# Rotating the latent-attention queries half by half, and transposing score maxima seven matmul groups after their reduction

## The chip, the cores and the metric

One core of a Trainium2 chip runs the whole program. The metric is the device time of one execution in microseconds (us). Three runs of the kernel before gave 1178.66, 1180.37 and 1183.4 us; the median is 1180.37.

## The reference, cut to what matters

Two layers run over a sequence of 1024 positions and a width of 1024. In each layer one projection feeds three mixers: retention, latent attention (MLA, 8 heads) and gated linear attention. Each is gated by a silu, and one output matrix follows. The change touches MLA:

```python
q = (rms_norm(q_lat, q_norm_w) @ w_uq).reshape(b, s, MLA_HEADS, MLA_NOPE + MLA_ROPE)
q_nope = q[..., :MLA_NOPE]
q_pe = rope(q[..., MLA_NOPE:], pos)
...
sc = (jnp.einsum('bqhd,bkhd->bhqk', qn, k_nope)
      + jnp.einsum('bqhd,bkd->bhqk', qp, k_pe)).astype(jnp.float32) * scale
mask = key_chunk[None, :] <= q_chunk[:, None]
sc = jnp.where(mask, sc, -jnp.inf)
p = jax.nn.softmax(sc, axis=-1).astype(v.dtype)
```

with `rope` returning `[x1*cos - x2*sin, x2*cos + x1*sin]`. Of each query's 96 columns, 64 ("nope") are used as they are and 32 are rotated.

## The kernel before

Float32 products are made of three matmuls: each operand is split into a high part and the rest, and `mm3` (L556 to L558) sums high*high, high*low and low*high into a PSUM bank. A "group" below is such a set of matmuls that ends in a `tick()`.

The order of TensorE's (PE's) instructions is written by hand, in the order of the Python calls. VectorE (DVE), ScalarE (ACT) and GpSimd (POOL) get their orders from a scheduler; SyncE (SP) starts all transfers, in one queue. Long side jobs are generators, *tasks*: each says after how many ticks of the main stream its next piece is to be put in, and `drain` puts in all that is left at once. In `layer()` the stretch that matters runs so:

- retention's core (`ret_core`) is a task, with one step about every 6 ticks. A step's matmuls (L790 to L834) need from DVE decay products (`retc_ram`, L793), a key product (`retc_rks`, L804) and states (`mq_rst`, L823, L825), and from POOL scaled queries (`retc_rqs`, L798).
- `mla_queries` is a generator that is called twice. The first part makes the rotary queries, two tiles for each half of the sequence (512 positions), and copies them to SBUF (`qx`). Then rz0, a gate projection, runs. The second part rotates both halves (`q_rope`: L732 to L737 on DVE, a cast L1118, the low part on POOL L1119, writes to DRAM L1121) and makes eight nope groups, each evicted by `pair_out` (L1106 on ACT, L1107 on DVE, writes L1109). These groups use PSUM pool `pj`, which has two banks. Then comes rz1.
- POOL also splits weights (L457) for the projections that come next: `wrz` for rz0 and rz1, `wgk` after them.
- `mla_max` is a task that finds, for each head and 128 queries, the maximum of each score row from the high parts: matmuls (L1243) into two sets of PSUM banks, each reduced by DVE (L1245) into a column of `mx`. Twelve such matmuls make one head, with 128 to 512 columns. A piece comes every 1.15 ticks (`MAXW`). The generator `close` then sums up a head's columns (`m8`, L1211), waits for some ticks, and transposes `m8` on PE (L1215) into a row in DRAM (L1217, L1218). It is called before the third block of the next head; for the last head it is a task of its own.
- `drain(big)` puts in what is left of the maxima, behind gate projection mz3 and ahead of the values (`mv`, evicted by L1189) and the attention itself.

Of the kernel before, what the change touches and what calls it, by code (L numbers as in the profile page):

```python
# [162 lines left out]
class Builder:  # L163
# [903 lines left out]
    def mla_queries(self, l, ql, tab):  # L1067

        nc = self.nc
        w, wn = self.weight((l, "uq"))  # L1070
        self.lab = "mq_"
        x = [[], []]
        for hf in range(2):
            for i in range(2):
                ps = self.ps("pj")
                self.uq_mtile(w, ql, i, hf, ps)
                x[hf].append(self.pt(name="qx"))
                nc.scalar.copy(x[hf][i], ps)
        yield
        for hf in range(2):  # L1080
            self.q_rope(l, x[hf], hf, *tab[hf])
        self.lab = "mq_"
        for pr in range(4):
            for hf in range(2):
                ps = self.ps("pj")
                self.uq_mtile(wn, ql, pr, hf, ps)
                self.pair_out(self.qn[l], pr, hf, ps)

    def mla_keys(self, l, kvl):
        (wh, wl), = self.weight((l, "ukvk"))  # L1090
        self.lab = "mk_"
        for pr in range(4):
            for hf in range(2):
                ps = self.ps(("pj", "s")[hf])
                g, cs = kvl[hf], slice(128 * pr, 128 * pr + 128)
                self.mm3(ps, wh[:, cs], wl[:, cs], g[:, 0, :], g[:, 1, :], True, True)
                self.tick()
                self.pair_out(self.kn[l], pr, hf, ps)
        for hf in range(2):
            self.nc.sync.dma_start(self.ld[l][hf], kvl[hf].bitcast(F32))  # L1100
# [92 lines left out]
    def mla_max(self, l):  # L1193

        nc = self.nc
        self.lab = "mmax_"
        sets = [{n: self.sl(dt=F32R, name="mx" + n) for n in "qk"} for _ in range(2)]
        for st in sets:
            for i, n in enumerate("kq"):
                nc.sync.dma_start(st[n][96:104, :].bitcast(F32), self.mrows[i, 1:9])  # L1200
            nc.sync.dma_start(st["k"][64:96, :].bitcast(F32), self.kr[l][0])

        def load(h):
            self.lab = "mmax_"
            for n in "qk":
                self.head_rows(l, h, n, 0, sets[h % 2][n])

        def close(h, mx):
            self.lab = "mmax_"
            m8 = self.sm([128, 8])  # L1210
            nc.vector.tensor_reduce(m8, mx, AX.X, ALU.max)  # L1211
            yield 4
            self.lab = "mmax_"
            ps = self.ps()
            nc.tensor.matmul(ps[0:8, 0:128], m8, self.cst("ident"), start=True, stop=True)  # L1215
            mr = self.smp.tile([8, 128], F32R, tag="mr", name=self.nm("mr"), bufs=2)
            nc.scalar.activation(mr, ps[0:8, 0:128], AF.Copy, scale=-1.0)  # L1217
            nc.sync.dma_start(self.mxd[l][h].rearrange("o (a b) -> (o a) b", a=8), mr.bitcast(F32))  # L1218

        load(0)  # L1220
        done = None
        for h in range(MH):
            yield MAXW
            st = sets[h % 2]
            if h + 1 < MH:
                load(h + 1)
            self.lab = "mmax_"
            mx = self.smp.tile([128, 8, 2], F32, tag="mx", name=self.nm("mx"), bufs=2)
            nc.gpsimd.memset(mx, NEG)
            for i in range(8):  # L1230
                n = 128 * (i + 1)
                for j in range((n + 511) // 512):
                    if i or j:
                        yield MAXW
                    if i == 2 and done:
                        yield from close(*done)
                        done = None
                        yield MAXW
                    self.lab = "mmax_"
                    w = min(512, n - 512 * j)  # L1240
                    ps = self.ps(self.maxp[self.nmx % len(self.maxp)])
                    self.nmx += 1
                    nc.tensor.matmul(ps[:, :w], st["q"][0:104, 128 * i:128 * i + 128],  # L1243
                                     st["k"][0:104, 512 * j:512 * j + w], start=True, stop=True)
                    nc.vector.tensor_reduce(mx[:, i, j:j + 1], ps[:, :w], AX.X, ALU.max)  # L1245
            done = (h, mx)
        self.task(close(*done), 8)

    def mla_scores(self, h, hf, j):
# [337 lines left out]
```

## Time and profile before

| what | value |
|---|---|
| median of three runs | 1180.37 us |
| the profiled execution's own time | 1183.94 us |
| its span | 1182.2 us |
| mean granted TensorE clock | 0.978 of 2.4 GHz |
| PE busy | 1118.6 us (95%) |
| DVE busy | 785.9 us (66%) |
| ACT busy | 596.2 us (50%) |
| POOL busy | 525.8 us (44%) |

The span is that of the profiled execution, from its first to its last instruction. Busy times count each engine by itself, and they overlap. An idle stretch is put down to the instruction that released the waiting one. The granted clock is a share of full speed: 1.00 is 2.4 GHz, 0.50 is 1.2 GHz. Layer 0 and layer 1 run the same program, about 568 us apart.

### The profile page before, as it was taken

What the parts mean: (1) busy time and instruction counts of PE and PEld (TensorE: products, weight loads), DVE (VectorE), ACT (ScalarE), POOL (GpSimd) and SP (SyncE); (2) the same over time, 40 slices, a digit from 0 to 9 for tenths busy, and PEclk for the clock granted to TensorE, in tenths of its full rate; (3) what the DMA queues carried; (4) which work ended last, traced back from release to release, by engine and by line L of the source; (5) the groups of instructions that cost most, each with busy time, mean ns of one, the idle gap of its engine ahead of it and who ended that gap; (6) DMA issues with size and microseconds to landing.
All of it is one profiled execution on the core that took longest, in us unless ns stands there. A gap on an engine that the chain in (4) does not pass through costs nothing.

```text
span 1182.2 us, 16973 instructions
## 1 busy us (share of the span) xinstructions
PE 1118.6 (95%) x5968; PEld 933.9 (79%) x5968; DVE 785.9 (66%) x1366; ACT 596.2 (50%) x1164; POOL 525.8 (44%) x459
## 2 busy tenths in 40 slices
PE   6999996899999999999999999969999999999996
PEld 3878985688878788887787898748888878888896
DVE  6866666568765656868875476474866565686754
ACT  6434342243554678863543434324355557886431
POOL 0055152445433446683565333335453344668620
PEclk8899998899999999999999999989999999999999
DMA  9725661662137534238443356155211653424722
GB/s 370 257 87 161 203 223 54 213 194 73 41 96 216 130 90 108 64 134 311 178 167 101 113 169 239 38 213 150 63 59 41 199 130 90 108 63 156 255 88 72
DMA packets 65585, 169.01 MB, mean 143 GB/s; under 512 B 10262, under 2 KB 13334, under 8 KB 65500
## 3 DMA queue, kind: packets, MB, share of 16 engines
q1 hardware_dynamic: 65500, 167.93, 44.8%
q8 instruction: 47, 0.77, 0.3%
q14 instruction: 38, 0.31, 0.1%
HBM read 125.36 MB, written 38.41 MB: 139 GB/s over the span
## 4 chain that ended last, share of the span: by engine, by line
PE 75%; DVE 12%; DMA 5%; ACT 4%; issue 3%; POOL 1%; SPq 0%; DVEq 0%; POOLq 0%; ACTq 0%
PE mhead_psacc L1294 3%; PE mhead_psacc L1292 3%; PE mhead_psacc L1293 3%; PE pmz_pspj L556 3%; PE pmz_pspj L557 2%; PE pmz_pspj L558 2%; DMA ada_aw<-awc 2%; DVE mmax_mx L1245 2%; PE wo_pss L558 2%; PE wo_pspj L556 2%; PE wo_pss L556 2%; PE wo_pss L557 2%; PE wo_pspj L558 2%; PE wo_pspj L557 2%; PE mhead_pss L1260 2%
## 5 line engine op out<-in xcount | busy, mean ns | idle before, releaser
L457 POOL TENSOR_TENSOR wwo_wl<-wwo_wst,wwo_wh 128x1024 fp32r<-128x1024 f32 x27 | 69.4, 2575 | 39.0 <-ACT wwo_wh L456 38.9
L1245 DVE TENSOR_REDUCE mmax_mx<-mmax_psmm 128x1 f32<-128x512 f32 (+1 forms) x96 | 57.4, 598 | 34.9 <-PE mmax_psmm L1243 33.9
L1269 POOL TENSOR_TENSOR mhead_wh<-mhead_p,mhead_wh 128x384 fp32r<-128x384 f32 (+1 forms) x48 | 57.9, 1207 | 45.5 <-DVE mhead_wh L1268 39.9
L576 DVE SCALAR_TENSOR_TENSOR ada_aw<-ada_aw,silrow 128x512 f32<-128x512 f32 x64 | 60.6, 966 | 18.6 <-DMA ada_aw<-awc 18.4
L1274 DVE TENSOR_TENSOR mhead_ph<-mhead_pss,mhead_ph 128x512 fp32r<-128x512 f32 x48 | 33.0, 688 | 36.2 <-ACT mhead_pss L1273 35.7
L556 PE MATMUL pmz_pspj<-mkh_h,wmz_wh 128*128 128x512 f32 x128 | 53.3, 417 | 0.0
L1269 POOL TENSOR_TENSOR mhead_wl<-mhead_p,mhead_wl 128x128 fp32r<-128x128 f32 (+1 forms) x48 | 35.8, 746 | 34.7 <-DVE mhead_wl L1268 34.7
L557 PE MATMUL pmz_pspj<-mkh_h,wmz_wh 128*128 128x512 f32 x128 | 50.9, 397 | 0.0
L558 PE MATMUL pmz_pspj<-mkh_h,wmz_wl 128*128 128x512 f32 x128 | 50.6, 395 | 0.0
L556 PE MATMUL mq_pspj<-latn_lat,wuq_wh 128*128 128x512 f32 x48 | 21.6, 450 | 26.0 <-DVE mq_pl L1107 25.6
L558 PE MATMUL wo_pspj<-gran_mx,wwo_wl 128*128 128x512 f32 (+1 forms) x120 | 44.3, 369 | 1.9 <-POOL wwo_wl L457 1.9
L556 PE MATMUL wo_pss<-gran_mx,wwo_wh 128*128 128x512 f32 (+1 forms) x120 | 44.5, 371 | 0.0
L556 PE MATMUL wo_pspj<-gran_mx,wwo_wh 128*128 128x512 f32 (+1 forms) x120 | 44.5, 371 | 0.0
L557 PE MATMUL wo_pss<-gran_mx,wwo_wh 128*128 128x512 f32 (+1 forms) x120 | 44.1, 368 | 0.0
L557 PE MATMUL wo_pspj<-gran_mx,wwo_wh 128*128 128x512 f32 (+1 forms) x120 | 44.1, 368 | 0.0
L558 PE MATMUL wo_pss<-gran_mx,wwo_wl 128*128 128x512 f32 (+1 forms) x120 | 44.1, 368 | 0.0
L457 POOL TENSOR_TENSOR wrk_wl<-wrk_wst,wrk_wh 128x1024 fp32r<-128x1024 f32 x3 | 8.0, 2682 | 79.5 <-ACT wrk_wh L456 79.5
L600 ACT ACTIVATE ssq_sq<-ssq_x 128x512 f32<-128x512 f32 (+1 forms) x31 | 16.6, 534 | 50.9 <-DVE ssq_x L1371 50.9
L605 DVE TENSOR_TENSOR ssq_sq<-ssq_sq,ssq_sq 128x512 f32<-128x512 f32 (+1 forms) x30 | 30.9, 1029 | 13.6 <-ACT ssq_sq L600 13.6
L1272 ACT ACTIVATE mhead_ph<-mhead_pss 128x512 fp32r<-128x512 f32 x48 | 28.6, 596 | 17.8 <-PE mhead_pss L1262 17.3
L1243 PE MATMUL mmax_psmm<-mmax_mxk,mmax_mxq 104*128 104x512 f32 (+1 forms) x96 | 35.5, 370 | 2.0 <-DVE mmax_mx L1245 1.5
L556 PE MATMUL pv_pspj<-wgv_wh,mkh_h 128*128 128x256 f32 x128 | 37.0, 289 | 0.0
(560 smaller groups left out, 4124.7 us busy)
## 6 DMA issues: line engine op xcount, KB each, us to landing
ada_aw<-awc SPq DMA_DIRECT2D x64, 256.0 KB
wwo_wst<-wo SPq DMA_DIRECT2D x32, 512.0 KB
aw<-awc SPq DMA_DIRECT2D x11, 512.0 KB
x<-xT SPq DMA_DIRECT2D x8, 512.0 KB
kn<-mk_ph SPq DMA_DIRECT2D x16, 256.0 KB
kn<-mk_pl SPq DMA_DIRECT2D x16, 256.0 KB
qn<-mq_ph SPq DMA_DIRECT2D x16, 256.0 KB
qn<-mq_pl SPq DMA_DIRECT2D x16, 256.0 KB
```

The lines of the kernel that those rows point to most:

```text
L457: (eng or nc.gpsimd).tensor_tensor(lo, src, hi.bitcast(F32), ALU.subtract)
L556: mm(ps, lh, rh, start=start, stop=False)
L557: mm(ps, lh, rl, start=False, stop=False)
L558: self.last = mm(ps, ll, rh, start=False, stop=stop)
L576: step = nc.vector.scalar_tensor_tensor(v, v, 1.0, self.silrow[:, cs], ALU.mult, ALU.mult, accum_out=t[:, 2 * j + i:2 * j + i + 1])
L1243: nc.tensor.matmul(ps[:, :w], st["q"][0:104, 128 * i:128 * i + 128], st["k"][0:104, 512 * j:512 * j + w], start=True, stop=True)
L1245: nc.vector.tensor_reduce(mx[:, i, j:j + 1], ps[:, :w], AX.X, ALU.max)
L1269: nc.gpsimd.tensor_tensor(pl, p, ph.bitcast(F32), ALU.subtract)
L1274: nc.vector.tensor_tensor(pl, s, ph.bitcast(F32), ALU.subtract)
L1292: mm(acc[:, o], vh, ph, start=(j == 0), stop=False, skip_group_check=True)
L1293: mm(acc[0:64, o], vl, ph, start=False, stop=False, skip_group_check=True)
L1294: mm(acc[:, o], vh, pl, start=False, stop=last, skip_group_check=True)
```

## The change

The rotation of the first half is issued in the first part of `mla_queries`, right behind that half's two tiles, ahead of rz0; the rotation of the second half is issued behind the eight nope groups. In `close`, the transposition of a head's maxima comes seven ticks after their last reduction instead of four.

```diff
--- before.py
+++ after.py
@@ -1076,15 +1076,17 @@
                 self.uq_mtile(w, ql, i, hf, ps)
                 x[hf].append(self.pt(name="qx"))
                 nc.scalar.copy(x[hf][i], ps)
+            if hf == 0:
+                self.q_rope(l, x[hf], hf, *tab[hf])
+                self.lab = "mq_"
         yield
-        for hf in range(2):
-            self.q_rope(l, x[hf], hf, *tab[hf])
         self.lab = "mq_"
         for pr in range(4):
             for hf in range(2):
                 ps = self.ps("pj")
                 self.uq_mtile(wn, ql, pr, hf, ps)
                 self.pair_out(self.qn[l], pr, hf, ps)
+        self.q_rope(l, x[1], 1, *tab[1])
 
     def mla_keys(self, l, kvl):
         (wh, wl), = self.weight((l, "ukvk"))
@@ -1209,7 +1211,7 @@
             self.lab = "mmax_"
             m8 = self.sm([128, 8])
             nc.vector.tensor_reduce(m8, mx, AX.X, ALU.max)
-            yield 4
+            yield 7
             self.lab = "mmax_"
             ps = self.ps()
             nc.tensor.matmul(ps[0:8, 0:128], m8, self.cst("ident"), start=True, stop=True)
```

Lines from L1079 on are two further on in the changed kernel. Three places show what moves.

DVE around the nope groups, before (`mrope` and `mq_qx` are the rotation, `mq_pl` the evictions), from the end of the second half's rotation:

```order
L737 TENSOR_TENSOR mq_qx_1610<-mq_qx_1610,mrope_rb_1785 128x512
L735 TENSOR_TENSOR mq_qx_1570<-mq_qx_1570,mrope_ra_1784 128x512
L1118 CAST mrope_qrh_1792<-mq_qx_1570 128x512
L1118 CAST mrope_qrh_1798<-mq_qx_1610 128x512
L793 TENSOR_TENSOR retc_ram_1817<-retc_pss_1811,cst 128x2x128
L793 TENSOR_TENSOR retc_ram_1817<-retc_pss_1812,cst 128x2x128
L804 TENSOR_TENSOR retc_rks_1826<-retc_psmm_1823,cst 128x256
L862 TENSOR_REDUCE hnorm_sm_1845<-hnorm_hsq_1843 128x8
L1107 TENSOR_TENSOR mq_pl_1856<-mq_pspj_1804,mq_ph_1855 128x512
L1107 TENSOR_TENSOR mq_pl_1869<-mq_pspj_1861,mq_ph_1868 128x512
```

DVE in the changed kernel, from retention's second step on:

```order
L804 TENSOR_TENSOR retc_rks_1550<-retc_psmm_1547,cst 128x256
L732 TENSOR_TENSOR mrope_ra_1563<-mq_qx_1561,pv_tab_1323 128x512
L733 TENSOR_TENSOR mrope_rb_1564<-mq_qx_1552,pv_tab_1323 128x512
L736 TENSOR_TENSOR mq_qx_1561<-mq_qx_1561,pv_tab_1322 128x512
L734 TENSOR_TENSOR mq_qx_1552<-mq_qx_1552,pv_tab_1322 128x512
L737 TENSOR_TENSOR mq_qx_1561<-mq_qx_1561,mrope_rb_1564 128x512
L735 TENSOR_TENSOR mq_qx_1552<-mq_qx_1552,mrope_ra_1563 128x512
L823 COPY mq_rst_1532<-retc_psmm_1616 64x64 x2
L823 COPY mq_rst_1533<-retc_psmm_1616 64x64 x2
L1120 CAST mrope_qrh_1571<-mq_qx_1552 128x512
L1120 CAST mrope_qrh_1577<-mq_qx_1561 128x512
L793 TENSOR_TENSOR retc_ram_1605<-retc_pss_1599,cst 128x2x128
```

The rotation of the first half moved from behind rz0 to between two steps of retention, with that step's state copies among it and the next step's products behind. That of the second half stands behind the last two evictions `mq_pl`, with two small norm rows and three state updates in it, and ahead of the last two `retc_ram`.

POOL at the weight splits of rz0 and rz1, before:

```order
L457 TENSOR_TENSOR wrz_wl_1518<-wrz_wst_1461,wrz_wh_1517 128x1024
L798 TENSOR_TENSOR retc_rqs_1588<-prk_rh_666,cst 128x128
L798 TENSOR_TENSOR retc_rqs_1588<-prk_rh_671,cst 128x128
L457 TENSOR_TENSOR wrz_wl_1614<-wrz_wst_1521,wrz_wh_1613 128x1024
L798 TENSOR_TENSOR retc_rqs_1647<-prk_rh_666,cst 128x128
```

and in the changed kernel:

```order
L457 TENSOR_TENSOR wrz_wl_1518<-wrz_wst_1461,wrz_wh_1517 128x1024
L457 TENSOR_TENSOR wrz_wl_1634<-wrz_wst_1521,wrz_wh_1633 128x1024
L1121 TENSOR_TENSOR mrope_qrl_1572<-mq_qx_1552,mrope_qrh_1571 128x512
L1121 TENSOR_TENSOR mrope_qrl_1578<-mq_qx_1561,mrope_qrh_1577 128x512
L798 TENSOR_TENSOR retc_rqs_1608<-prk_rh_666,cst 128x128
```

The two splits now follow each other, and the first half's two low parts stand behind them and ahead of the scaled queries. The second half's two low parts stand likewise ahead of the last pair of `retc_rqs`, behind the split of `wgk`.

PE at `drain(big)` in layer 0, changed kernel, from the seventh head's last maxima (`mxk_2241`) to the last head's (`mxk_2243`):

```order
L1245 MATMUL mmax_psmm_3833<-mmax_mxk_2241,mmax_mxq_2240 128x512
L1245 MATMUL mmax_pss_3836<-mmax_mxk_2241,mmax_mxq_2240 128x512
L1245 MATMUL mmax_psmm_3841<-mmax_mxk_2243,mmax_mxq_2242 128x128
L1245 MATMUL mmax_pss_3844<-mmax_mxk_2243,mmax_mxq_2242 128x256
L1217 MATMUL mmax_psmm_3849<-cst,mmax_sm_3847 8x128
L1245 MATMUL mmax_psmm_3854<-mmax_mxk_2243,mmax_mxq_2242 128x384
L1245 MATMUL mmax_pss_3857<-mmax_mxk_2243,mmax_mxq_2242 128x512
L1245 MATMUL mmax_psmm_3860<-mmax_mxk_2243,mmax_mxq_2242 128x512
```

Before, ten maxima stood in one piece there, all of the last head. Now ten of the head before it, two of the last head, the transposition and the same ten stand in one piece, 22 maxima, ahead of the values.

## Rows read from the trace of the kernel before

**Rows 1.** Page, part 1: busy us, share of the span, instructions, by engine.

```profile
PE 1118.6 (95%) x5968; PEld 933.9 (79%) x5968; DVE 785.9 (66%) x1366; ACT 596.2 (50%) x1164; POOL 525.8 (44%) x459
```

**Rows 2.** Waits of PE: line, what released it, us in total, times, longest.

```profile
PE mq_pspj L556 <- DVE mq_pl L1107: 25.6, 4, 12.5
...
PE mmax_psmm L1215 <- DVE mmax_sm L1211: 3.7, 3, 2.1
...
PE prz_pspj L556 <- DVE mq_pl L1107: 2.3, 2, 1.2
```

**Rows 3.** Timeline of PE, `mq_pspj` and the drain's start: start, us, operation, [idle before].

```profile
210.13 0.80 PE L556 MATMUL mq_pspj<-latn_lat,wuq_wh 128*128 128x512 f32 x1 [12.53 <-DVE mq_pl L1107]
...
214.14 0.53 PE L556 MATMUL mq_pspj<-latn_lat,wuq_wh 128*128 128x512 f32 x1
...
400.44 0.39 PE L558 MATMUL pmz_pspj<-mkh_h,wmz_wl 128*128 128x512 f32 x1
...
400.67 0.34 PE L1243 MATMUL mmax_psmm<-mmax_mxk,mmax_mxq 104*128 104x384 f32 x1
...
778.07 0.79 PE L556 MATMUL mq_pspj<-latn_lat,wuq_wh 128*128 128x512 f32 x1 [12.53 <-DVE mq_pl L1107]
...
780.80 0.51 PE L556 MATMUL mq_pspj<-latn_lat,wuq_wh 128*128 128x512 f32 x1
```

**Rows 4.** Timeline of DVE during PE's first stall.

```profile
201.15 1.75 DVE L732 TENSOR_TENSOR mrope_ra<-mq_qx,pv_tab 128x512 f32<-128x512 f32 x1
...
204.49 0.68 DVE L736 TENSOR_TENSOR mq_qx<-mq_qx,pv_tab 128x512 f32<-128x512 f32 x1
...
207.01 0.76 DVE L1118 CAST mrope_qrh<-mq_qx 128x512 fp32r<-128x512 f32 x2
...
208.81 0.68 DVE L862 TENSOR_REDUCE hnorm_sm<-hnorm_hsq 128x8 f32<-128x512 f32 x1
```

**Rows 5.** Timelines of ACT (first row) and DVE where the halves now go.

```profile
170.41 0.59 ACT L1078 COPY mq_qx<-mq_pspj 128x512 f32<-128x512 f32 x1 [1.44 <-PE mq_pspj L558]
...
174.80 0.97 DVE L823 COPY mq_rst<-retc_psmm 64x64 f32<-64x64 f32 x4
...
227.26 1.29 DVE L1107 TENSOR_TENSOR mq_pl<-mq_pspj,mq_ph 128x512 fp32r<-128x512 f32 x2
```

**Rows 6.** Timeline of POOL around the three places.

```profile
170.52 2.39 POOL L457 TENSOR_TENSOR wrz_wl<-wrz_wst,wrz_wh 128x1024 fp32r<-128x1024 f32 x1
...
201.04 2.97 POOL L1119 TENSOR_TENSOR mrope_qrl<-mq_qx,mrope_qrh 128x512 fp32r<-128x512 f32 x2 [3.31 <-DVE mrope_qrh L1118]
...
228.49 2.39 POOL L457 TENSOR_TENSOR wgk_wl<-wgk_wst,wgk_wh 128x1024 fp32r<-128x1024 f32 x1 [9.60 <-ACT wgk_wh L456]
```

**Rows 7.** Timeline of PE: retention's steps that follow, and the first maxima.

```profile
180.43 0.61 PE L815 MATMUL retc_psmm<-pv_v,retc_rks 128*128 128x128 f32 x4
...
181.72 0.66 PE L834 MATMUL retc_psacc<-mq_rst,retc_rqs 128*128 128x128 f32 x4
...
237.57 1.00 PE L830 MATMUL retc_psacc<-pv_v,retc_ram 128*128 128x64 f32 x8
...
251.71 0.23 PE L1243 MATMUL mmax_psmm<-mmax_mxk,mmax_mxq 104*128 104x128 f32 x1
```

**Rows 8.** Timeline of PE behind the drain, layer 0.

```profile
407.44 0.39 PE L556 MATMUL mv_pspj<-wukvv_wh,pmz_lat 128*128 128x256 f32 x1 [1.52 <-DVE pmz_vl L1189]
```

**Rows 9.** Timeline of DVE in the drain, first reduction and the values' eviction.

```profile
401.05 0.56 DVE L1245 TENSOR_REDUCE mmax_mx<-mmax_psmm 128x1 f32<-128x384 f32 x1 [0.38 <-PE mmax_psmm L1243]
...
406.71 1.28 DVE L1189 TENSOR_TENSOR pmz_vl<-mv_pspj,pmz_vh 128x512 fp32r<-128x512 f32 x2
```

**Rows 10.** Windows: us, busy of PE, PEld, DVE, ACT, POOL, PEclk, DMA share, GB/s.

```profile
404.00:407.00 3.00, 1.92 (x14) 1.67 (x13) 3.00 (x6) 1.59 (x3) 0.57 (x1) 1.00 0.95 249
...
27.50:30.00 2.50, 1.45 (x4) 1.16 (x5) 2.37 (x4) 1.80 (x3) 0.00 (x0) 0.50 1.02 419
...
40.00:42.50 2.50, 2.50 (x16) 2.16 (x15) 2.50 (x5) 0.00 (x0) 0.00 (x0) 0.93 1.03 383
```

## The prediction

> **What bounds the kernel now.** I read the page's busy times first. TensorE (PE) is busy 95% of the span, VectorE (DVE) 66%, GpSimd (POOL) 44% [rows 1]. So a change pays only where it shortens PE's idle time, or costs where it adds some. The next view is therefore the list of what PE waits for [rows 2]. Its largest entry is the one that the change aims at: the third group of the nope queries (`mq_pspj`) waits for the eviction `mq_pl`, 25.6 us in 4 waits, the longest 12.5. The transposition of maxima, which the change also touches, waits 3.7 us in 3 places. In the same list the first group of rz1 (`prz`) waits 2.3 us, in 2 waits, for the last `mq_pl`: a plain wait for one of the two `pj` banks, with nothing foreign in between. That is what a nope group costs when only its own eviction is ahead.
>
> PE's timeline gives the place: idle 12.53 us before 210.13, the same before 778.07 in layer 1 [rows 3]. What DVE does meanwhile is the third view [rows 4]: the rotation of both halves, 16 instructions, whose last casts end at 207.77; behind them retention's products and a norm's sum (208.81), and only then the evictions. The rotation stands ahead of the first eviction in DVE's order, and PE has two banks, so it fills both and stops. The stall has a tail: after it the matmuls come 0.43 us apart instead of 0.23 (400.44 to 400.67 in the same group of rows). In layer 0 nine intervals take 4.01 us (210.13 to 214.14), which at 0.23 would be 2.07; in layer 1 six take 2.73 instead of 1.38 [rows 3]. So 1.9 + 1.35 = 3.3 us more.
>
> **The change, part by part** (both layers unless said). No arithmetic is added: each instruction counts, moved.
>
> *1. The stall goes.* With no rotation between rz0 and the evictions, the 2 x 12.53 us and the tail of 3.3 go: -28.4 us. What is late next is the third group's own bank. I price it by the row that has just this wait, `prz` on `mq_pl`: +2.3 us. Ends: 1.2 (one of the two waits) and 4.6 (a norm's sum ahead costs as much again).
>
> *2. The early half.* It now stands on DVE between two steps of retention, and its two low parts on POOL ahead of the scaled queries (`rqs`) of the next step. DVE has its input at 171.00 (the second copy of `qx` ends) [rows 5]. But POOL is splitting a weight from 170.52 to 172.91 [rows 6], and the second split of that size, which stood behind `rqs`, now follows at once. What a DVE operation does beside POOL's is in two groups [rows 4, 6]: the one at 201.15 took 1.75 us and ended 0.4 behind POOL's first low part (201.04 and half of 2.97), while those from 204.49 on, with POOL idle, take 0.68 and start 0.63 apart. So the first multiplication ends at about 173.3, the second, held by the second split, at 175.8, four more at 178.3, four state copies (0.97) at 179.3, then casts, decay products and the key product (207.01 to 208.81, 1.80) at 181.1. PE wants the key product at 180.43 [rows 7]: 0.7 us late. On POOL the low parts start behind the first cast (179.7) and take 2.97, `rqs` an estimated 0.8 (two of 128 columns, by the low part's 1.49 for 512): 183.5. PE wants it at 181.72 + 0.7: another 1.1. Together 1.8 us a layer, +3.6. Ends per layer: 0.3 (only one multiplication is held) and 3.5 (three).
>
> *3. The late half.* It starts behind the last eviction, at 227.26 + 1.29 = 228.55 [rows 5], again beside a weight split (228.49 to 230.88) [rows 6]. One held operation to 231.3, five at 0.63 to 234.4, two small norm operations and three state updates (about 1.3, estimated from the copies) to 235.7, casts and decay products to some 237.3: in time for PE's last values step at 237.57 [rows 7]. The low parts are not: first cast 236.1, plus 2.97, plus 0.8 for the last `rqs`, 239.9, where PE wants it within a microsecond of 237.57, at 238.3. 1.6 us a layer, +3.2. Ends: 0 and 3. SyncE's queue is crossed too: the late half's four writes now stand ahead of the loads for the first head of maxima. Those can issue from about 240; PE first uses them at 251.71 [rows 7], some 12 us on, so I cost it at nothing; with that cover gone, each microsecond would show.
>
> *4. The transposition seven groups later.* Its waits go, all but some tenths: -3.4 us. Ends: -3.7 and 0, if DVE's column products, which also stand ahead of `m8`, hold it anyway.
>
> *5. What those groups cost.* The maxima are a task paid in groups. Three groups more in each of seven heads leave 22 maxima instead of 10 for the drain before the values, with one transposition among them. In the drain nothing covers them: before, PE began at 400.67 [rows 3] and stood 1.52 us at 407.44 for `pmz_vl`, which is behind the last reduction [rows 8]; DVE's ten reductions and one 0.60 us gate operation ran almost without a break from 401.05 to `pmz_vl` at 406.71 [rows 9], so ten cost 5.06. Of the twelve more, ten are of the same widths (six of 512 columns, two of 384, one of 256, one of 128), and the two others, 256 and 128 wide, take about 0.5 by their share: 5.6 us, plus an estimated 0.9 for a sum, the transposition and the refill between. PE saves their 4608 columns elsewhere: at 0.23 us for 512, 2.1. So 5.6 + 0.9 - 2.1 = 4.4 a layer, +8.8. Ends per layer: 3.3 and 5.5.
>
> *Sum:* -28.4 + 2.3 + 3.6 + 3.2 - 3.4 + 8.8 = -13.9 us. It is made against the profiled execution, whose own time is 1183.94 us (span 1182.2); this lies 3.57 above the median of the three runs, 1180.37. From there the sum gives **1166.5 us**. All bounds together reach from -23.7 to +0.
>
> **Rivals.**
>
> *A. The drain costs TensorE its clock (slower).* In the first stage PE, fed slowly by DVE, was busy 1.45 of 2.5 us (27.5 to 30) and was granted 0.50, 1.2 GHz, and full speed, 2.4 GHz, came back only in the window from 40 [rows 10]: at least 10 us at the lower level, and up to 15 with the windows' edges, say 12.5. Against it: in the old drain PE was busy 1.92 of 3 us (404 to 407) and kept 1.00. The new drain is over twice as long, and no row shows one of that length. If the clock falls in it, the reductions still set the pace (0.43 is under 0.60), but the second half of the values' 24 matmuls loses about 1.4 us, and 12.5 us at half speed 6.25: 7.7 a layer, 15.3 in all, so +1.4: 1181.8 us. It decides where the lower level outlasts the drain by more than 11 us in both layers; by 17 us, the time is over 1186.3.
> The Trainium skill, "TensorE: Matmul & The Clock Gate", section "A second HAM failure mode: psum-queue depth-cycling", says that a PE which pauses briefly between groups while it cycles through PSUM banks can swing between its two clock levels, and lose throughput between bursts. That rule speaks against this change: the drain is such a cycle, over two sets of banks. By the rule the sum would be rival A's; by the row at 404 it is mine.
>
> *B. POOL holds the whole rotation (no change).* If each of the six operations of each half took 1.75, the early half would end 5.1 us late instead of 1.8 (6 x 1.75 from 171.0, then as above), the late half 6.0 instead of 1.6: +15.4, so +1.5, 1182 us. It decides if all six meet a POOL operation. Against it: POOL has but two splits near the early half and one near the late.
>
> *C. The bounds add up (no change).* Drain, both halves and the remaining waits at their upper ends: up to 1180 us.
>
> *D. Nothing of it lands on PE (better).* Both halves slip into DVE's gaps, the drain costs 3.3: about 1157 us.
>
> *E. The change doesn't do what it says*, DVE's scheduler putting the rotation back ahead of the evictions: 1180 us. The instruction orders exclude it.
>
> **How the numbers follow.** A measurement of this kernel tells 0.5%, 5.9 us, from no change: faster is below 1174.5, slower above 1186.3. My forecast 0.72, D 0.04: faster 0.76. A 0.10, of which 0.06 is beyond 1186.3; B 0.07, C with what is left of E 0.07: same 0.18, slower 0.06. The range reaches up to 1181 to take in C and leaves out most of A and B, about 0.15; below it ends at 1159, short of D.
>
> **What would show it.** Right: no `mq_pspj` wait over 2 us; clock 1.00 through the nope groups; new PE waits of one to two microseconds on `rqs` or `rks` at the steps that follow each half; 22 maxima in one piece, and the values' third group some 13 us behind the drain's start instead of 6.8. Wrong in part 2 or 3: no such waits, or ones over 3 us. Wrong in part 5: it comes under 11 us behind, or the clock leaves 1.00 behind it (A). The forecast falls if a wait of several microseconds stands anywhere among the nope groups.

## The result, and the profile after

The changed kernel takes 1185.03 us (median of 20 runs) beside 1182.37 for the kernel before (20 runs, in the same series). The ratio is 1.0033, with a 95% interval of 1.002 to 1.0045: slower by a third of a per cent, where 1.2% faster was forecast. The profiled executions have spans of 1182.8 us and 1182.2 us.

What the forecast spoke of first did happen. This is the list of what PE waits for in the changed kernel (line, releaser, total us, times, longest):

```profile
PE mmax_psmm L1245 <- DVE mmax_mx L1247: 5.9, 6, 2.3
...
PE mmax_psmm L1217 <- DVE mmax_sm L1213: 4.0, 2, 2.0
PE mq_pspj L556 <- DVE mq_pl L1109: 3.7, 4, 1.6
PE glac_psacc L1009 <- DVE mmax_mx L1247: 3.4, 2, 1.7
...
PE retc_pss L790 <- DVE retc_ram L793: 2.4, 2, 1.3
PE mmax_pss L1245 <- DVE mmax_mx L1247: 2.1, 2, 1.1
```

Against [rows 2], `mq_pspj` on `mq_pl` fell from 25.6 us to 3.7. The wait of the transposition did not go: 3.7 us in 3 places became 4.0 in 2. The waits for the reductions of maxima have grown, from 1.5 us in 5 places before to three lines of 5.9, 3.4 and 2.1. New are 2.4 us for retention's decay products. PE is busy longer with the same instructions (page, part 1, against [rows 1]):

```profile
PE 1128.0 (95%) x5968; PEld 942.6 (80%) x5968; DVE 796.7 (67%) x1366; ACT 596.6 (50%) x1164; POOL 529.5 (45%) x459
```

9.4 us more PE time for the same 5968 matmuls has two sources. Some ran at the lower clock, as shown below. Others stood apart, and then each counts with its whole length (0.39 us for 512 columns), where in a dense row they start 0.23 us apart and overlap. To see where the time went, I set the same matmul in both traces side by side (us; the difference is after minus before, and its change from row to row is what a stretch gained or lost):

| first matmul of | before | after | difference | stretch |
|---|---|---|---|---|
| layer 0: queries | 166.44 | 162.82 | -3.62 | the first stage, untouched by the change |
| gk, behind the queries and retention | 243.01 | 229.88 | -13.13 | **-9.5** |
| gz, behind gv | 288.39 | 280.31 | -8.08 | **+5.1** |
| mz0, behind the gated attention | 339.91 | 333.65 | -6.26 | +1.8 |
| the drain | 400.67 | 391.38 | -9.29 | -3.0 |
| scores behind the values | 408.98 | 407.44 | -1.54 | **+7.8** |
| layer 1: queries | 733.71 | 732.90 | -0.81 | +0.7 |
| gk | 810.37 | 799.89 | -10.48 | **-9.7** |
| gz | 854.42 | 848.76 | -5.66 | **+4.8** |
| mz0 | 905.92 | 899.92 | -6.00 | -0.3 |
| the drain | 963.00 | 955.49 | -7.51 | -1.5 |
| scores behind the values | 971.31 | 972.12 | +0.81 | **+8.3** |

The -3.6 us of the first stage are a difference between two executions (other runs below have other values there); without them the pair stands at about +4 us, which is the measured 0.33%. So the queries gained 19.2 us, and from gk to the scores about 23 were lost again: 9.9 in gv and 16.1 in the drain, less 3.0 in the two stretches between. These two should have become shorter by more than that, as part of their maxima moved into the drain; the first of them, the gated attention, is a third place where time was lost.

**In gv** PE stops twice (timeline of PE, after):

```profile
272.33 0.50 PE L1245 MATMUL mmax_pss<-mmax_mxk,mmax_mxq 104*128 104x512 f32 x1 [1.07 <-DVE mmax_mx L1247]
...
275.87 0.48 PE L1245 MATMUL mmax_psmm<-mmax_mxk,mmax_mxq 104*128 104x128 f32 x1 [2.33 <-DVE mmax_mx L1247]
```

DVE's timeline there shows what stands ahead of the two reductions that PE waits for (at 271.85 and 275.12), the decay factors of the gated attention (`gla_prep`), first one operation pair of 1.7 us, then a block:

```profile
270.12 1.70 DVE L939 TENSOR_TENSOR glap_gkp<-pgk_gk,glap_gz 64x512 f32<-64x512 f32 x2
271.85 0.42 DVE L1247 TENSOR_REDUCE mmax_mx<-mmax_pss 128x1 f32<-128x256 f32 x1
272.31 0.93 DVE L930 TENSOR_TENSOR glap_gkm<-pgk_gk,glap_gel 128x256 f32<-128x256 f32 x1
...
273.49 0.83 DVE L931 TENSOR_TENSOR glap_gkm<-pgk_gk,glap_gt 128x256 f32<-128x256 f32 x1
274.25 0.84 DVE L935 TENSOR_TENSOR glap_gka<-pgk_gk,glap_gt 64x256 f32<-64x256 f32 x2
275.12 0.69 DVE L1247 TENSOR_REDUCE mmax_mx<-mmax_psmm 128x1 f32<-128x512 f32 x1
```

The block, 2.8 us from 272.31 on, is in the kernel before as well, 2.7 us long and with four reductions behind it (DVE, then PE, timelines of before):

```profile
285.29 0.81 DVE L930 TENSOR_TENSOR glap_gkm<-pgk_gk,glap_gel 128x256 f32<-128x256 f32 x1
...
287.99 0.69 DVE L1245 TENSOR_REDUCE mmax_mx<-mmax_psmm 128x1 f32<-128x512 f32 x1
```

```profile
285.31 0.38 PE L1243 MATMUL mmax_pss<-mmax_mxk,mmax_mxq 104*128 104x256 f32 x1
...
290.06 0.39 PE L1215 MATMUL mmax_psmm<-cst,mmax_sm 128*8 128x128 f32 x2 [0.81 <-DVE mmax_sm L1211]
```

There the pause of the second head's transposition lay on the block: from 285.31 to 290.06 PE asked for no bank of maxima. With the first head's pause three groups longer, all later maxima stand 18 matmuls of gv further back, about 2 us at 0.12 us each. So PE still has some to issue while DVE is in the block, and stops. The clock follows (windows, after; columns as in [rows 10]):

```profile
272.00:275.00 3.00, 1.21 (x7) 0.97 (x7) 2.96 (x6) 0.00 (x0) 1.68 (x2) 0.94 0.28 83
275.00:278.00 3.00, 2.13 (x10) 2.13 (x11) 2.81 (x7) 0.00 (x0) 0.07 (x1) 0.50 0.53 141
278.00:281.00 3.00, 3.00 (x14) 2.90 (x14) 0.42 (x1) 0.46 (x2) 0.05 (x1) 0.50 0.00 0
281.00:284.00 3.00, 3.00 (x13) 2.46 (x13) 0.00 (x0) 0.86 (x1) 2.06 (x1) 0.93 0.00 0
```

Behind a stretch with 1.21 us of work in 3, PE was granted 0.50 (1.2 GHz) until about 281, though it had work all the time from 276 on. The two waits are 3.4 us; the stretch lost 5.1. The rest is the clock: from 276.14 to 280.31 the matmuls start 0.21 us apart instead of 0.12, which makes 19 of them about 1.9 us longer.

**In the gated attention**, between gz and mz0, PE waits once more in each layer, for an accumulator bank that a reduction of maxima still reads (timeline of PE, then windows, after):

```profile
311.03 1.10 PE L1009 MATMUL glac_psacc<-pv_v,pgz_gat 128*128 128x64 f32 x8 [1.68 <-DVE mmax_mx L1247]
...
878.98 1.10 PE L1009 MATMUL glac_psacc<-pv_v,pgz_gat 128*128 128x64 f32 x8 [1.69 <-DVE mmax_mx L1247]
```

```profile
311.00:314.00 3.00, 2.97 (x14) 2.49 (x15) 0.59 (x3) 0.97 (x2) 1.52 (x4) 0.69 0.74 160
...
879.00:882.00 3.00, 3.00 (x22) 2.80 (x22) 1.30 (x5) 1.35 (x4) 1.46 (x3) 1.00 0.74 164
```

In layer 0 the clock falls behind this wait, in layer 1 it does not. The stretch has 15 maxima instead of 23, which by 0.23 us for 512 columns is 1.3 us less, and the transposition's wait of 0.81 us is gone from it. It should have been 2.1 us shorter; it is 1.8 longer in layer 0 and 0.3 shorter in layer 1. So it lost about 3.9 and 1.8 us (an estimate; in layer 0 some 0.5 of it is still the low clock behind gv).

**In the drain** (timeline of PE, after; the first maxima, the last ahead of the transposition, the transposition, the values' first and third group, the first score):

```profile
391.38 0.34 PE L1245 MATMUL mmax_psmm<-mmax_mxk,mmax_mxq 104*128 104x384 f32 x1
...
395.75 0.39 PE L1245 MATMUL mmax_pss<-mmax_mxk,mmax_mxq 104*128 104x256 f32 x1
398.16 0.60 PE L1217 MATMUL mmax_psmm<-cst,mmax_sm 128*8 128x128 f32 x2 [2.02 <-DVE mmax_sm L1213]
...
403.03 0.41 PE L556 MATMUL mv_pspj<-wukvv_wh,pmz_lat 128*128 128x256 f32 x1
...
405.88 0.39 PE L556 MATMUL mv_pspj<-wukvv_wh,pmz_lat 128*128 128x256 f32 x1 [0.68 <-DVE pmz_vl L1191]
...
407.44 0.40 PE L1262 MATMUL mhead_pss<-pmz_stkqh,pmz_stkkh 105*128 105x512 f32 x1
```

It takes 16.06 us instead of 8.31, 16.63 instead of 8.31 in layer 1. The transposition stands 2.02 us in the middle of it, while DVE catches up, and the clock falls here too (windows, after):

```profile
395.00:398.00 3.00, 0.90 (x3) 0.37 (x2) 3.00 (x8) 0.63 (x1) 0.96 (x1) 0.92 0.88 224
398.00:401.00 3.00, 2.84 (x8) 1.88 (x8) 1.69 (x5) 0.27 (x1) 0.35 (x2) 0.50 0.94 219
401.00:404.00 3.00, 2.99 (x10) 2.35 (x10) 3.00 (x8) 0.00 (x0) 0.00 (x0) 0.50 0.04 6
404.00:407.00 3.00, 2.32 (x18) 2.12 (x18) 2.10 (x4) 1.27 (x3) 1.97 (x5) 0.95 0.00 0
```

### The profile page after: what moved, and what is told of

Read it like the earlier page. It is cut to its first block, busy times and chain, and to the rows that moved or that the text cites. A ratio compares the mean times of both kernels' runs of the same rounds, so it can differ in the third digit from the quotient of the medians.

```text
span 1182.8 us, 16979 instructions
## 1 busy us (share of the span) xinstructions
PE 1128.0 (95%) x5968; PEld 942.6 (80%) x5968; DVE 796.7 (67%) x1366; ACT 596.6 (50%) x1164; POOL 529.5 (45%) x459
## 4 chain that ended last, share of the span: by engine, by line
PE 75%; DVE 12%; ACT 4%; DMA 4%; issue 3%; POOL 1%; SPq 0%; DVEq 0%; ACTq 0%; POOLq 0%
PE mhead_psacc L1296 3%; PE mhead_psacc L1294 3%; PE mhead_psacc L1295 3%; PE wo_pspj L558 2%; PE wo_pspj L556 2%; PE wo_pspj L557 2%; PE pmz_pspj L556 2%; PE wo_pss L557 2%; PE wo_pss L556 2%; PE wo_pss L558 2%; PE pmz_pspj L557 2%; PE pmz_pspj L558 2%; DVE mmax_mx L1247 2%; PE mhead_pss L1263 2%; PE mhead_pss L1262 2%
## 5 line engine op out<-in xcount | busy, mean ns | idle before, releaser
L1247 DVE TENSOR_REDUCE mmax_mx<-mmax_psmm 128x1 f32<-128x512 f32 (+1 forms) x96 | 57.3, 596 | 26.4 <-PE mmax_psmm L1245 25.6
L576 DVE SCALAR_TENSOR_TENSOR ada_aw<-ada_aw,silrow 128x512 f32<-128x512 f32 x64 | 62.0, 986 | 18.5 <-DMA ada_aw<-awc 18.2
L1245 PE MATMUL mmax_psmm<-mmax_mxk,mmax_mxq 104*128 104x512 f32 (+1 forms) x96 | 38.9, 408 | 6.6 <-DVE mmax_mx L1247 5.9
L1247 DVE TENSOR_REDUCE mmax_mx<-mmax_pss 128x1 f32<-128x256 f32 (+2 forms) x72 | 36.5, 507 | 7.5 <-PE mmax_pss L1245 6.8
```

Of the source, the lines that this page charges most:

```text
L576: step = nc.vector.scalar_tensor_tensor(v, v, 1.0, self.silrow[:, cs], ALU.mult, ALU.mult, accum_out=t[:, 2 * j + i:2 * j + i + 1])
```

## The experiments

Theory 1: the two edits have separate accounts, the rotation gains about 19 us, the later transposition loses about 22, in gv (by where the maxima fall) and in the drain (by how many it holds). Theory 2: the stall gave DVE a lead that the next stretch lives on, so the loss comes from the rotation's move. Base of the diffs is the changed kernel unless said.

**1. The rotation alone.**

```diff
-            yield 7
+            yield 4
```

> The rotation in two parts, with the transposition after 4 groups as before. Theory 1 (the two parts of the change have separate accounts): between the same landmarks the changed kernel gained 9.5 and 9.7 us up to the end of the queries, and lost it again among the maxima, so this kernel is 19 us faster than the one before, about 1163 us, the drain holds 10 maxima at clock 1.00 and no wait of PE for a maxima's reduction is over 0.8 us. Theory 2 (the stall gave VectorE a lead that the next stretch lives on, so taking it away costs there whatever the transposition does): 5 to 9 us faster, with waits of 1 to 2.5 us on reductions in the stretch of gv still there.

Measured: 1163.04 us, ratio 0.9827 (0.979 to 0.9864). A second time, in experiment 9: 1161.98 us, 0.9834 (0.9813 to 0.9855). Waits of PE and the drain's windows:

```profile
PE mmax_psmm L1217 <- DVE mmax_sm L1213: 3.7, 3, 2.1
...
PE mmax_psmm L1245 <- DVE mmax_mx L1247: 0.7, 4, 0.2
```

```profile
389.00:392.00 3.00, 2.66 (x15) 1.98 (x16) 3.00 (x7) 1.24 (x3) 0.66 (x2) 1.00 0.58 164
392.00:395.00 3.00, 1.48 (x13) 1.27 (x12) 2.66 (x6) 1.42 (x3) 1.49 (x3) 1.00 0.96 219
```

No wait of PE for a maxima's reduction (`mmax_mx`) is longer than 0.2 us, and the drain takes 8.30 us at clock 1.00. Theory 1 holds, theory 2 falls. By its medians this is also the fastest kernel of the study, though the intervals of several later ones reach into its own.

**2. The later transposition alone**, on the kernel before:

```diff
-            yield 4
+            yield 7
```

> The rotation as before, both halves behind rz0, with the transposition after 7 groups. Theory 1 (two separate accounts): 20 to 23 us slower than before, about 1204 us, with waits of 1.1 and 2.3 us on reductions in gv, clock 0.50 behind them, a drain of 22 maxima that ends at clock 0.50, and the waits of 12.5 us in the queries still there. Theory 2 (the loss needs the earlier queries as well): 0 to 10 us slower and no wait over 1 us in gv.

Measured: 1207.04 us, ratio 1.022 (1.0193 to 1.0248). Waits:

```profile
PE mq_pspj L556 <- DVE mq_pl L1107: 25.6, 4, 12.5
PE mmax_psmm L1243 <- DVE mmax_mx L1245: 5.5, 5, 2.3
...
PE mmax_psmm L1215 <- DVE mmax_sm L1211: 4.0, 2, 2.0
PE glac_psacc L1009 <- DVE mmax_mx L1245: 3.4, 2, 1.7
```

The old stall and the new waits stand side by side: the loss doesn't need the earlier queries. 2.2% is some 26 us, 22.8 to 29.3 by the interval; the difference between the changed kernel and experiment 1 is 22.0. In this run as in the changed kernel, PE also waits 1.7 us a layer in the gated attention.

An earlier run under this heading was the kernel before, unchanged. Its expectation was the same in substance:

> The rotation as before, with the transposition after 7 groups. Theory 1: 20 to 23 us slower than before, about 1203 us: the waits on reductions in gv of 1.1 and 2.3 us, clock 0.50 behind them, a drain of 22 maxima that takes about 16 us instead of 8.3 and ends at clock 0.50; the waits of 12.5 us in the queries stay. Theory 2: 0 to 10 us slower, with no wait over 1 us in gv, as VectorE keeps its lead.

It measured 1183.55 us, ratio 1.0011 (0.9993 to 1.0029), and says nothing of the theories. It shows what the comparison gives for no change at all.

**3. Seven groups for the first head only.**

```diff
-            yield 7
+            yield 7 if h == 0 else 4
```

> Rotation in two parts; 7 groups only for the first head's transposition, 4 for the others. The drain holds 10 maxima again. Theory 1a (the pause of the first head sets where the following maxima meet the decay factors of the gated attention on VectorE): 9 to 10 us slower than with 4 for all, about 1173 us, with the waits of 1.1 and 2.3 us and clock 0.50 in gv, and clock 1.00 in the drain. Theory 1b (all of the loss is the longer drain): the same as with 4 for all, within 2 us, about 1163 us.

Measured: 1169.99 us, ratio 0.9889 (0.9854 to 0.9923). One head's pause brings back both waits in gv, in both layers, and the clock behind them:

```profile
PE mmax_psmm L1245 <- DVE mmax_mx L1247: 5.5, 5, 2.3
...
PE mmax_pss L1245 <- DVE mmax_mx L1247: 2.2, 2, 1.1
```

```profile
275.00:278.00 3.00, 1.93 (x9) 1.94 (x10) 2.94 (x7) 0.00 (x0) 0.00 (x0) 0.52 0.59 165
278.00:281.00 3.00, 3.00 (x15) 2.90 (x15) 0.50 (x2) 0.26 (x1) 0.11 (x1) 0.50 0.00 0
```

7 us more than experiment 1 (9 to 10 expected, under 2 by the rival): the place in gv is a cause of its own. By the landmarks gv loses 5.6 and 5.4 us against experiment 1; a part comes back later, as the wait of 2.1 us for the fourth head's transposition is gone in layer 0.

**4. Seven groups for all but the first.**

```diff
-            yield 7
+            yield 4 if h == 0 else 7
```

> Rotation in two parts; 4 groups for the first head's transposition, 7 for the seven others: a drain of 19 maxima. Theory 1a: no wait over 1 us in gv, so what is left is the drain, some 10 to 13 us slower than with 4 for all, about 1175 us, with clock 0.50 in the drain. Theory 1b (all in the drain): 19 to 22 us slower than with 4 for all, about 1183 us.

Measured: 1170.55 us, ratio 0.9887 (0.9843 to 0.993), 7.5 us more than experiment 1. No wait in gv is over 0.61 us, the drain of 19 takes 14.49 us (14.56 in layer 1), and its clock falls to 0.50. That is theory 1a, with less loss than expected. One new wait, in layer 0 only, shows that a pause can miss one block and meet another, here DVE's column products (L576, one of them 2.84 us):

```profile
347.35 0.52 PE L1245 MATMUL mmax_psmm<-mmax_mxk,mmax_mxq 104*128 104x512 f32 x1 [3.06 <-DVE mmax_mx L1247]
```

**5. Seven groups with denser maxima.**

```diff
-MAXW = 1.15
+MAXW = 0.95
```

> The changed kernel, 7 groups, with the maxima paced at 0.95 group instead of 1.15. In the orders the transpositions then stand at nearly the same places as with 4 groups, and the drain holds 10 maxima. Theory 1a (what costs is where the maxima fall and how many the drain holds): within 5 us of the kernel with 4 groups, 1163 to 1168 us, clock 1.00 in the drain. Rival (the denser maxima or the pause of 7 cost by themselves, as VectorE can't take a reduction every 0.95 group): 1172 us or more, with waits on reductions outside gv.

Measured: 1164.34 us, ratio 0.9859 (0.9839 to 0.9878). With the pause of seven kept and nothing changed but the pace, nearly the whole loss is gone. The drain holds 10 maxima and takes 8.74 us, at clock 1.00. In gv one wait of 1.5 us a layer is left, and the clock stays at 1.00 behind it. The drain's windows:

```profile
391.00:394.00 3.00, 2.66 (x16) 2.08 (x16) 3.00 (x8) 0.70 (x2) 0.00 (x0) 1.00 0.91 208
394.00:397.00 3.00, 1.47 (x13) 1.27 (x12) 2.51 (x6) 1.37 (x4) 1.63 (x3) 1.00 0.03 7
```

So it is not the seven groups as such, but what they do to the places and the count; this run changes both at once and does not part them.

**6 and 7. Fewer maxima in the drain: three groups, or 1.05 with four.**

```diff
-            yield 7
+            yield 3
```

> Rotation in two parts, transposition after 3 groups: 4 maxima in the drain instead of 10, everything behind the first head's pause one group earlier. Theory 1a: the drain loses six reductions of VectorE (3.0 us) and PE's own time for them comes back elsewhere (1.0), so 4 us faster than with 4 groups, about 1159 us, if nothing new collides in gv. Rival (the place in gv decides, and one group is enough to lose it): waits of 1 us and more on reductions or on the transposition, 1163 to 1170 us.

```diff
-MAXW = 1.15
+MAXW = 1.05
...
-            yield 7
+            yield 4
```

> Rotation in two parts, transposition after 4 groups, maxima paced at 1.05 instead of 1.15: 2 in the drain. Theory 1a: eight reductions fewer in the drain, 4.0 us of VectorE against 1.4 of PE, 2.6 a layer: 5 us faster than with 1.15, about 1158 us, if nothing collides. Rival: the maxima meet the decay factors in gv, 1163 to 1170 us.

Measured: 1168.22 us, ratio 0.9891 (0.9859 to 0.9922), and 1165.74 us, 0.9868 (0.9845 to 0.989). Neither beats experiment 1; the rival holds in both. With 1.05 the maxima meet the decay factors in gv (waits of 1.3 and 1.2 us, at 267.20 and 826.01). One group fewer brings waits of 1.0 and 1.1 us in gv, and these two, for the values' eviction and, behind the gated attention, for a reduction:

```profile
PE mv_pspj L556 <- DVE pmz_vl L1191: 4.0, 4, 1.8
...
PE hout_psacc L874 <- DVE mmax_mx L1247: 2.3, 2, 1.5
```

**8. Two groups for the last four heads only.**

```diff
-            yield 7
+            yield (4 if h <= 3 else 2)
```

> Rotation in two parts; transposition after 4 groups for heads 0 to 3, so that everything in gv and the gated attention stays where it is with 4, and after 2 for heads 4 to 7, whose maxima run beside the gate projections, where VectorE is little loaded: 5 maxima in the drain instead of 10. Five reductions fewer in the drain are 2.5 us of VectorE against 0.9 of PE: 1 to 1.6 us a layer, so 2 to 3 us faster than with 4 for all, about 1160.5 us. Rival: the transposition itself then waits for its sum, or the saving is lost to the wait of the values for their eviction: no difference.

Measured: 1165.91 us, ratio 0.9872 (0.9847 to 0.9897). No gain. gv is almost untouched, and the drain holds 5. But the stretch ahead of it, where the five maxima now are, takes 2.6 and 1.1 us more than in experiment 1, and the drain gives back only some 1.2 us a layer, because the values wait longer for their eviction, as PE is there sooner than DVE:

```profile
PE mv_pspj L556 <- DVE pmz_vl L1191: 5.6, 2, 2.8
```

**9. Experiment 1 again**, beside it:

> Rotation in two parts, transposition after 4 groups for all, a second time, on the same chip as the kernel with 2 for the late heads: 1163 us, a ratio of 0.983 to the kernel before.

Measured: 1161.98 us, ratio 0.9834, as said above; 1163 and 0.983 were expected.

**10. The second half's rotation ahead of the nope groups again**, with four groups.

```diff
+        self.q_rope(l, x[1], 1, *tab[1])
         self.lab = "mq_"
         for pr in range(4):
...
-        self.q_rope(l, x[1], 1, *tab[1])
...
-            yield 7
+            yield 4
```

> Rotation of the first half early, of the second half ahead of the nope groups again; transposition after 4 groups. If the stall is VectorE's time for the rotation that stands ahead of the first eviction, half of the rotation leaves about half of the stall: one wait of 6 us a layer instead of 12.5, and the late half's waits behind the queries (1.6 us a layer) are gone. About 1170 to 1174 us. If the stall were set by something else ahead of the evictions (the norm's sum, the states), it stays near 12 us or goes altogether.

Measured: 1175.75 us (one run). The stall is halved, as the eight DVE operations of one half are:

```profile
PE mq_pspj L556 <- DVE mq_pl L1109: 12.5, 4, 6.0
```

**11. The drain with PE fed.** The kernel does surplus work: 22 matmuls more a layer, whose results nobody reads.

```diff
                     nc.vector.tensor_reduce(mx[:, i, j:j + 1], ps[:, :w], AX.X, ALU.max)
+                    if getattr(self, "filling", False):
+                        fp = self.ps("acc")
+                        nc.tensor.matmul(fp, st["q"][0:104, 0:128], st["k"][0:104, 0:512], start=True, stop=True)
...
+        self.filling = True
         self.drain(big)
+        self.filling = False
```

> The changed kernel with one more matmul of 512 columns, into an accumulator bank that nobody reads, behind each of the 22 maxima in the drain: PE is fed while VectorE reduces. From the drain's first maxima to the first score matmul behind the values the changed kernel takes 16.1 us, against 8.3 before, and the granted clock is 0.50 from 398 to 404. Theory A (the drain is paced by VectorE, the clock is a small part of it): the clock stays at 1.00 or nearly, and the stretch takes 14 to 15 us. Theory B (the fallen clock is what makes the drain dear): clock 1.00 and 12 us or less. If the clock falls all the same, the run tells nothing.

In layer 0 the clock stayed at 1.00 and the stretch took 15.29 us instead of 16.06:

```profile
396.00:399.00 3.00, 2.62 (x13) 1.92 (x12) 3.00 (x8) 1.27 (x3) 0.37 (x1) 1.00 0.85 184
399.00:402.00 3.00, 1.82 (x9) 1.15 (x10) 2.15 (x7) 0.28 (x2) 1.38 (x2) 1.00 0.90 243
402.00:405.00 3.00, 3.00 (x16) 2.52 (x15) 3.00 (x8) 0.00 (x0) 0.00 (x0) 1.00 0.32 66
```

In layer 1 it fell all the same, to 0.61 between 966 and 969, so that half says nothing. By layer 0, one execution, the clock is some 0.8 us of the drain's 7.8 (1.3 if the 16.63 us of layer 1 in the changed kernel are set beside it): theory A, though at 15.29 us a little over its 14 to 15. The surplus matmuls may cost some tenths themselves, so the share of the clock may be a little larger. The whole run took 1187.07 us (one run).

## Why the prediction was wrong

*The stall and what is late next (part 1): right.* No stall is left, the clock is 1.00 through the queries, and the third group waits 1.56 us where 1.15 a layer was taken, inside its ends. That the stall was DVE's rotation is shown by experiment 10 as well.

*Early and late half (parts 2 and 3): right in size, not in place.* The early half cost 1.7 us in layer 0 and 1.0 in layer 1 (1.8 forecast), but PE waited for a decay product that still held a bank of scores (`retc_pss` on `retc_ram`), not for the key product or `rqs`. The late half cost 1.7 and 1.5 (1.6 forecast), in waits of at most 0.4 us each. So the sign that was named for these parts, waits of one to two microseconds on `rqs` or `rks`, did not come: the longest on `rqs` is 0.37 us. Parts 1 to 3 add up to -19.3 us; the landmarks say -19.2, and experiment 1 measures -19.1 and -18.9 by its two pairs of medians.

*The transposition (part 4): wrong.* The step read "its waits go": they went where they were, but the drain has a new one of 2.0 us a layer. `drain` puts in all pieces at once, so a pause of seven groups is no pause there.

*The maxima (part 5): this step failed.* It priced the drain and nothing else. Parts 4 and 5 together were +5.4 us; the difference of the changed kernel to experiment 1 is 22.0. The 22 maxima did stand in one piece, and the values' third group came 14.5 us behind its start, where some 13 were forecast. So the drain itself was mis-sized a little: 7.8 and 8.3 us longer, which is 5.7 and 6.2 beyond PE's saved 2.1, where the term was 4.4 with an upper end of 5.5. What was missing altogether is gv, 5.1 and 4.8 us, and the gated attention, some 3.9 and 1.8 us: for neither had the sum a term. I had looked at the pause only as a distance between a head's sum and its transposition, and at its effect on the count. But the maxima are one chain of paced pieces: the first head's pause also moves every later piece, about 2 us, against other work on DVE. The trace of before had what was needed: DVE's block at 285.29, and PE's free stretch beside it. Experiment 3 brings the loss in gv back with this one pause alone, and experiment 5 takes most of it away with the pause kept.

*Rival A: half right.* The clock did fall in the drain, and in gv and (in layer 0) in the gated attention, which no rival named. But in the drain it stayed low for some 6 us in layer 0 and 9 in layer 1, not 12.5, and the drain's own pace by DVE hid most of it (about 1 us in experiment 11). The trace of before had a nearer row than the first stage, which the prediction passed over: behind the transposition's wait of 2.09 us (345 to 348, PE busy 0.91 of 3 us) the clock was 0.51 from 348 to 351 and 1.00 again in the next window. The rule that was cited beside rival A, in the Trainium skill, "TensorE: Matmul & The Clock Gate", section "A second HAM failure mode: psum-queue depth-cycling", agrees with the windows 395 to 404 in that PE paused between groups and was granted 0.50 then. But that PE's cycling brought the clock down is not shown: a single wait of 2.02 us lies there, the fall is in it, and the drain of ten in experiment 1 cycles likewise and stays at 1.00. Of the rule's consequence, lost throughput, the runs here show little in the drain, and some 2 us a layer in gv, behind two single waits.

Rival B counted six held operations of each half. Two are held in the early half (2.46 and 2.87 us, in layer 0) and one in the late half (2.88), as many as the forecast took. Rival C's bounds end at 1180 us, and the result lies beyond them. Rivals D and E played no part: the drain cost more, not less, and nothing of the rotation went back ahead of the evictions.

The result lies so near the time before only because a gain of 19 us and a loss of 22, from two edits with separate accounts, nearly cancel.

Experiments 3 and 4 lose 7.0 and 7.5 us, which together is 7.5 less than the changed kernel loses. The landmarks say where most of the rest is: between gz and mz0. Against experiment 1 this stretch, both layers together, is 1.4 us shorter in experiment 3 and 3.9 in experiment 4, but 1.5 longer in the changed kernel. That is 6.8 us more than the two pauses give one by one, and neither of the two runs has the wait of 1.7 us there; the three runs with seven groups for every head at the old pace have it. Why it takes both pauses to bring a reduction to that place stays open.

## What to carry to other kernels

A pause in a paced side task is a move of everything behind it: read, on the engine that serves it, what its later pieces will now meet, not only what the pause itself frees. A `drain` at the end collects all that the pauses pushed out, and there the slower engine sets the pace. And where a change holds two edits, price and run them apart: here one was worth 1.7%, and the other hid it.

## What the runs showed of the hardware that was not expected

- An idle PE is paid twice when the clock goes: 3.4 us of waits in gv cost 5.1 us in layer 0, with 0.50 granted until about 281, some 5 us after PE had full work again.
- How much idleness the clock stands is not told by the busy share of one stretch. At 1.48 us busy in 3 (experiment 1, 392 to 395) and 1.47 in 3 (experiment 5) it stayed at 1.00; it fell behind 1.21 in 3 (gv) and 0.90 in 3 (the drain), and in layer 1 of experiment 11 behind 1.48 in 3 (963 to 966). Even at the same place of the program it goes either way: with a wait of 2.09 us for the fourth head's transposition and 0.91 in 3 it fell to 0.51 in the kernel before (345 to 351) and stayed at 1.00 in experiment 1 (333 to 339). So part of a single execution's time is luck, and the clock's price is better read from several.
- DVE's evenness can matter more than its load: it is busy 66 to 67% of the span in both kernels, and one block of 2.8 us, met by maxima that come 2 us later, cost about 5 us a layer.
